# Hybrid decoder block on one core: gate projections of token groups two and three in float32r halves, gathers planned with other factors

## The chip, the cores and the metric

The kernel runs on one core of a Trainium2 chip. The metric is the device time of one execution in microseconds (us); less is better. The engines are TensorE (PE, matrix products; its weight loads are shown apart as PEld), VectorE (DVE), ScalarE (ACT), GpSimd (POOL), which here mostly issues the gathers, and SyncE (SP), which issues most loads. Each engine works through its own queue in order.

## The reference

One decoder layer over 1024 tokens of width 1024, all in float32. Three token mixers share a normalised input h; sigmoid gates merge their projections; an expert mixer follows.

```python
h = rms_norm(x, g_mix[l])
proj = h @ w_in[l]
...
y_sb = stick_breaking_attention(...) @ w_o_sb[l]
y_dil = dilated_mixture(...) @ w_o_dil[l]
y_mem = memory_attention(...) @ w_o_mem[l]
gates = jax.nn.sigmoid(h @ w_gate[l] + b_gate[l]).reshape(B, S, N_BRANCHES, D)
merged = gates[:, :, 0] * y_sb + gates[:, :, 1] * y_dil + gates[:, :, 2] * y_mem
x = x + merged @ w_out[l]
h2 = rms_norm(x, g_ffn[l])
x = x + peer_ffn(h2, w_peer_q[l], peer_subkeys[l], peer_u[l], peer_v[l])
```

In `peer_ffn` each of 8 heads of a token picks 16 of 16384 experts by product keys. For each chosen expert the row u is multiplied with h2, gelu and the softmax gate are applied, and the row v is added with that weight: 128 rows of u and 128 rows of v for each token.

## The kernel before

The 1024 tokens are eight blocks of 128. They pass through the dense part of the layer in three **groups** of two, three and three blocks (`GROUPS`, line 29). For each group `phase1` (line 1017) runs the stages one after the other: input norm, stick-breaking attention, dilated attention, memory attention, gating, output projection, second norm, expert selection. Weights come as 128 x 1024 blocks, one for each 128 output columns; `Weights` keeps three of them prepared in four buffers `w`.

**Two ways of multiplying.** A plain float32 product goes through `mm` (line 112) and leaves two records on PE, with its time at 4 cycles a column in the planner. In the other way both operands are split by `halves` (line 276): ACT copies the operand to float32r, which rounds it (hi), and DVE subtracts that from the operand (lo). Three products hi x hi, lo x hi and hi x lo then replace the one, through `mmr` (line 1193), one record each. `proj_T` (line 343) does either, by the type of the weight it gets. Only group one (`SPLIT`, line 42) uses halves in phase one; they are held in the gathers' row buffers u and v, which are idle until the first block is selected. The dense expert stage uses halves too.

**Gating** (`gating`, line 775) goes over eight column blocks and three branches. For each of the 24 pairs it computes the gate projection of h (1024 rows, eight products), Tanh on ACT, then the branch's own projection with w_o out of `oT` (four, two or four products), and combines the two on DVE. It yields after each of the two. `out_proj` follows.

**Experts.** Blocks 4 and 6 (`DENSE`) are computed densely, against all 16384 experts, by `dense` (line 1245) after the three groups. The other six blocks gather. A **step** is one u row and one v row for 128 partitions: two indirect DMAs on POOL, a product with sum on DVE (line 1151), and four PE products (line 1177). A block has 128 steps, so there are 768. PE's four times four products of four steps stand together, followed by two products that spread the next tokens' h2 (line 1090). There are five buffers for u rows and six for v rows, and a gather waits until its buffer is free.

**The planner** (the loop at the end of `block_kernel`) decides where in the program steps stand. It holds two clocks: `pe`, to which each piece of phase one adds its estimated PE time times `slow` and each step adds 700 ns, and `dma`, to which each adds its bytes by `bw`. While `dma` is ahead it takes another piece of phase one (or of the dense stage), otherwise a step. `SLOW` (line 39) has 1.38 for phase one and 1.1 for the dense stage, `BW` (line 38) 295 and 360 GB/s. So a smaller factor on a stage puts fewer steps into it, and a higher rate puts more steps into every stage. The scheduler below the planner keeps the written order on ACT and may move instructions of the other engines a little.

**The gate matrix** (`gate_matrix`, line 1203) builds the dense blocks' gates. For block 4 this happens during gating and output projection of group three, one or two pieces at each yield of these stages. It stages 1 MB tiles from `room` (line 1197), out of the pool `big` with three buffers, and stores them to memory; for block 6 they come from a pool with two buffers, `g`.

Other names: `qpad` (line 222) holds the padded queries of the attentions; its zero halves are written once. `k0`, `v` of the pool `kvp` are keys and values of the nearest dilated group, `pT` transposed probabilities; all are unused during gating. `sc` holds the selection's scores.

Of the kernel before, what the change touches and what calls it, by code (L numbers as in the profile page):

```python
# [7 lines left out]
F32 = mybir.dt.float32  # L8
# [29 lines left out]
BW = 295.0, 360.0  # L38
SLOW = 1.38, 1.1
# [38 lines left out]
def block_kernel(ctx: ExitStack, tc: tile.TileContext, io):  # L78
# [143 lines left out]
    qpad = const.tile([128, 6, NMAX], F32)  # L222
    for i in range(6):
        h0 = 64 if i % 2 == 0 else 0
        nc.vector.memset(qpad[h0:h0 + 64, i, :], 0.0)
# [25 lines left out]
    def weight_order(gidx):  # L251
# [9 lines left out]
        for pp in range(2):  # L261
            for g in range(3):
                for x in range(3):
                    yield "w_in", NB_SB + 6 * x + 2 * g + pp, every, split and x < 2
            for h in range(2):
                yield "w_in", NB_SB + 18 + 2 * pp + h, every, split
        for n in range(8):
            for br, (k0, nk) in enumerate(BR):
                yield "w_gate", br * 8 + n, every, split
                yield "w_o", n, slice(k0, k0 + nk), False  # L270
# [72 lines left out]
    def proj_T(w, h, n):  # L343

        p = bank()
        if type(w) is tuple:
            wh, wl = w
            for k in range(KD):
                hh, hl = (x[:, k % 4, :n] for x in h[1][k // 4])
                mmr(p[:, :n], wh[:, k, :], hh, start=k == 0, stop=False)  # L350
                mmr(p[:, :n], wl[:, k, :], hh, start=False, stop=False)
                mmr(p[:, :n], wh[:, k, :], hl, start=False, stop=k == KD - 1)
            return p
# [3 lines left out]
        return p  # L357

# [6 lines left out]
    def both(gidx, h, n):  # L365
# [4 lines left out]
        for k in range(0, KD, 4):  # L370
            parts.append(tuple(x.rearrange("p (k n) -> p k n", k=4) for x in spare()))
            halves(*(x[:, :, :n] for x in parts[-1]), (h[0] if type(h) is list else h)[:, k:k + 4, :n])
        return h, parts

# [44 lines left out]
    def stick_breaking(pipe, weights, hT, n0, G, oT):  # L419
        N = G * 128  # L420
        t0 = n0 * 128
# [127 lines left out]
    def dilated(pipe, weights, hT, n0, G, oT, between):  # L549
        N = G * 128  # L550
        t0 = n0 * 128
# [223 lines left out]
    def gating(pipe, weights, hT, N, oT, mT):  # L775

        for n in range(8):
            for br, (k0, nk) in enumerate(BR):
                p = proj_T(weights("w_gate", br * 8 + n), hT, N)
# [237 lines left out]
    def phase1(gidx, n0, G, out):  # L1017
# [34 lines left out]
        yield from out_proj(weights, mT, n0, G, x2)  # L1052
        h2T = [big.tile([128, 8, NS], F32, name="big") for _ in subs(G)]
# [143 lines left out]
    def room():  # L1197
# [3 lines left out]
        return big.tile([128, 64, 32], F32, name="big")  # L1201
# [186 lines left out]
    def rest():  # L1388
        n0 = built = 0
        odd = False  # L1390
        for g in range(len(GROUPS)):
            for stage in phase1(g, n0, GROUPS[g], ready):
                if stage and built < ND:
# [103 lines left out]
```

## Time and profile before

| | us |
|---|---|
| median of three runs | 3574.66 |
| lowest and highest run | 3574.15, 3581.68 |
| the profiled execution | 3564.13 |
| its span, first to last instruction | 3562.4 |

In the page's slices below, each column is a fortieth of the span (89 us) and each digit a busy share in tenths; the last row is what the DMA engines moved.

```profile
PE   6999879989999889999998999776779999999954
DVE  5444597565644469995656665788867677777654
DMA  4425659999899999989998999998999999999999
GB/s 151 140 84 182 221 210 342 336 342 340 318 405 392 403 361 348 331 329 356 328 351 292 391 386 401 350 326 338 399 384 391 365 382 382 390 383 373 349 380 377
```

Until about 484 us group one runs, with no gathers. Then follow group two with the first gathers (to 1387 us), group three (to 2411 us), the rest of the gate matrix (to 2652 us), the dense stage, and from 3396 us the gathers that are left. These borders are read from the first products of each stage on PE.

### The profile page before, as it was taken

What the parts mean: (1) busy time and instruction counts of PE and PEld (TensorE: products, weight loads), DVE (VectorE), ACT (ScalarE), POOL (GpSimd) and SP (SyncE); (2) the same over time, 40 slices, a digit from 0 to 9 for tenths busy, and PEclk for the clock granted to TensorE, in tenths of its full rate; (3) what the DMA queues carried; (4) which work ended last, traced back from release to release, by engine and by line L of the source; (5) the groups of instructions that cost most, each with busy time, mean ns of one, the idle gap of its engine ahead of it and who ended that gap; (6) DMA issues with size and microseconds to landing.
All of it is one profiled execution on the core that took longest, in us unless ns stands there. A gap on an engine that the chain in (4) does not pass through costs nothing.

```text
span 3562.4 us, 61070 instructions
## 1 busy us (share of the span) xinstructions
PE 3189.3 (90%) x22930; PEld 2359.5 (66%) x22930; DVE 2356.0 (66%) x6003; ACT 1371.6 (39%) x2747; POOL 1768.1 (50%) x1544
## 2 busy tenths in 40 slices
PE   6999879989999889999998999776779999999954
PEld 6889856656555766666565657654558888888720
DVE  5444597565644469995656665788867677777654
ACT  4443345554411214656544221322224444444410
POOL 0000036655566565766555655566645444544476
PEclk9989989999999999999999999887899999999965
DMA  4425659999899999989998999998999999999999
GB/s 151 140 84 182 221 210 342 336 342 340 318 405 392 403 361 348 331 329 356 328 351 292 391 386 401 350 326 338 399 384 391 365 382 382 390 383 373 349 380 377
DMA packets 346431, 1185.56 MB, mean 333 GB/s; under 512 B 38744, under 2 KB 80216, under 8 KB 326680
## 3 DMA queue, kind: packets, MB, share of 16 engines
q0 software_dynamic: 221184, 805.40, 59.6%
q1 hardware_dynamic: 102672, 337.95, 25.9%
q10 hardware_dynamic: 22280, 38.31, 2.8%
q8 instruction: 181, 2.97, 0.3%
q14 instruction: 114, 0.93, 0.1%
HBM read 1142.18 MB, written 39.32 MB: 332 GB/s over the span
## 4 chain that ended last, share of the span: by engine, by line
PE 60%; DVE 14%; DMA 14%; issue 5%; ACT 4%; POOL 2%; ACTq 0%; SPq 0%; POOLq 0%; DVEq 0%
PE bank L117 30%; PE bank L1195 21%; DMA u<-in_u,iT 7%; PE po L1177 7%; DVE u L1151 4%; DMA v<-in_v,iT 2%; PE pb L1090 2%; DMA b3d<-sp 1%; PE bank L121 1%; POOL u L1097 1%; POOL v L1097 1%; ACT L126 1%; DMA g<-gd 1%; ACT e L128 1%; DMA gd<-g 1%
## 5 line engine op out<-in xcount | busy, mean ns | idle before, releaser
L1097 POOL DMA_INDIRECT u<-in_u,iT x768 | 920.9, 1199 | 965.0 <-DVE i L865 487.7
L1097 POOL DMA_INDIRECT v<-in_v,iT x768 | 846.4, 1102 | 817.8 <-PE po L1177 644.5
L1151 DVE SCALAR_TENSOR_TENSOR u<-u,hb 128x1024 f32<-128x1024 f32 x768 | 927.0, 1223 | 437.6 <-ACT hb L128 274.3
L1177 PE MATMUL po<-v,wz 128*32 128x256 f32 x6144 | 443.7, 416 | 150.2 <-DMA v<-in_v,iT 83.2
L117 PE MATMUL bank<-wide,w 128*128 128x384 f32 x1536 | 520.8, 493 | 2.6 <-DMA w<-in_w_gate 2.6
L117 PEld LDWEIGHTS bank<-wide,w 128*128 128x128 f32 x1536 | 293.1, 193 | 202.7 <-issue 11.2
L1177 PEld LDWEIGHTS po<-v,wz 128*32 128x32 f32 x6144 | 181.8, 115 | 369.6 <-DMA v<-in_v,iT 115.7
L128 ACT ACTIVATE hb<-pb 128x512 f32<-128x512 f32 x384 | 208.2, 595 | 400.0 <-PE pb L1090 257.3
L117 PEld LDWEIGHTS bank<-w,wide 128*128 128x128 f32 x2304 | 263.0, 192 | 7.5 <-issue 2.3
L117 PE MATMUL bank<-w,wide 128*128 128x128 f32 x2304 | 265.3, 275 | 0.2 <-DMA w<-in_w_out 0.2
L1195 PE MATMUL bank<-hh,ul 128*128 128x256 f32 x848 | 240.0, 283 | 1.3 <-DVE ul L1275 1.3
L1195 PE MATMUL bank<-hh,uh 128*128 128x256 f32 x848 | 240.9, 284 | 0.0
L1195 PE MATMUL bank<-hl,uh 128*128 128x256 f32 x848 | 239.9, 283 | 0.0
L128 ACT ACTIVATE e<-bank 128x512 f32<-128x512 f32 (+2 forms) x208 | 109.6, 527 | 277.4 <-PE bank L117 249.3
L1195 PE MATMUL bank<-vh,wh 128*128 128x512 f32 x512 | 203.0, 403 | 2.2 <-ACT vh L128 2.2
L1195 PE MATMUL bank<-vl,wh 128*128 128x512 f32 x512 | 201.8, 394 | 2.4 <-DVE vl L1275 2.3
L1195 PE MATMUL bank<-vh,wl 128*128 128x512 f32 x512 | 199.5, 390 | 0.0
L126 ACT ACT_TABLE_LOAD x144 | 184.8, 1283 | 20.6 <-issue 8.4
L128 ACT ACTIVATE w<-bank 128x256 f32<-128x256 f32 x128 | 49.3, 385 | 366.0 <-PE bank L1195 285.1
L1275 DVE TENSOR_TENSOR vl<-vr,vh 128x1024 fp32r<-128x1024 f32 x128 | 157.1, 1227 | 31.8 <-ACT vh L128 31.8
L117 PE MATMUL bank<-big,w 128*128 128x128 f32 (+1 forms) x1024 | 175.9, 330 | 0.6 <-DMA w<-in_w_pq 0.6
L1195 PE MATMUL bank<-u 128*128 128x256 f32 x544 | 164.9, 303 | 10.2 <-ACT u L128 10.2
(297 smaller groups left out, 5887.9 us busy)
## 6 DMA issues: line engine op xcount, KB each, us to landing
ur<-in_uT SPq DMA_DIRECT2D x64, 1024.0 KB
vr<-in_vd SPq DMA_DIRECT2D x64, 1024.0 KB
w<-in_w_in SPq DMA_DIRECT2D x102, 512.0 KB
w<-in_w_gate SPq DMA_DIRECT2D x72, 512.0 KB
w<-in_w_pq SPq DMA_DIRECT2D x48, 512.0 KB
g<-gd SPq DMA_DIRECT2D x16, 1024.0 KB
w<-in_w_o SPq DMA_DIRECT2D x48, 256.0 KB
w<-in_w_out SPq DMA_DIRECT2D x24, 512.0 KB
```

What stands on the lines that cost most here:

```text
L117: nc.tensor.matmul(out, lhsT, rhs, **kw)
L121: nc.tensor.transpose(out, in_, ident)
L126: nc.scalar.preload_act_table_set(s)
L128: nc.scalar.activation(out, in_, f, **kw)
L1090: nc.tensor.matmul(pb, which[:, jj].rearrange("p q s -> p (q s)"), box["b3"][:, f], start=True, stop=True)
L1097: nc.gpsimd.indirect_dma_start(out=t, out_offset=None, in_=io[kind], in_offset=bass.IndirectOffsetOnAxis(ap=ap, axis=0))
L1151: nc.vector.scalar_tensor_tensor(u, u, 1.0, self.hb, op0=OP.mult, op1=OP.mult, accum_out=self.parts[:, i:i + 1])
L1177: nc.tensor.matmul(po[32 * k:32 * k + 32, h:h + 256], wz[:, i, :], v[:, 256 * k:256 * k + 256], start=jj == 0 and i == 0, stop=jj == QB - ...
L1195: nc.tensor.matmul(out, lhsT, rhs, **kw)
L1275: nc.vector.tensor_sub(lo, r[:, x], hi)
```

## The change

The gate projections of groups two and three are split into halves, all but the first of each group. The tokens' halves (`gate_tokens`) take three tiles of `big` and one of `sq`. The weights' halves (`gate_halves`) go by turns into the tile of `qpad` and into `k0`, `v` and two tiles `pT`. The weight of the next projection is split ahead of the present one, so a gate weight is loaded one place earlier. `qpad`'s zero halves are written anew after the output projection of group two. `room` takes its tiles from `sc`, which has two buffers, since `big` is taken. The planner's first rate becomes 330 GB/s, and its factor becomes 1.0 in gating and output projection (stages that yield 1); the other stages keep 1.38.

```diff
-BW = 295.0, 360.0
-SLOW = 1.38, 1.1
+BW = 330.0, 360.0
+SLOW = 1.38, 1.1, 1.0
...
+    def query_pad():
+
+        held_q[0] = const.tile([128, 6, NMAX], F32, name="qpad")
+        for i in range(6):
+            h0 = 64 if i % 2 == 0 else 0
+            nc.vector.memset(held_q[0][h0:h0 + 64, i, :], 0.0)
+        return held_q[0]
...
+        gate_blocks = [("w_gate", br * 8 + n, every, split) for n in range(8) for br in range(3)]
+        if not split:
+            yield gate_blocks.pop(0)
         for n in range(8):
-            for br, (k0, nk) in enumerate(BR):
-                yield "w_gate", br * 8 + n, every, split
+            for k0, nk in BR:
+                if gate_blocks:
+                    yield gate_blocks.pop(0)
                 yield "w_o", n, slice(k0, k0 + nk), False
...
+    def gate_tokens(hT, N):
+
+        a, b, c = (big.tile([128, 2048], F32, name="big").bitcast(F32R) for _ in range(3))
+        sq = tmp.tile([128, NMAX], F32, name="sq").bitcast(F32R)
+        rows = lambda t, o, m: t[:, o:o + m * NMAX].rearrange("p (k n) -> p k n", k=m)
+        hi = ((rows(a, 0, 5), 0, 5), (rows(b, 0, 3), 5, 3))
+        lo = ((rows(b, 3 * NMAX, 2), 0, 2), (rows(c, 0, 5), 2, 5), (rows(sq, 0, 1), 7, 1))
+        his, los = [], []
+        for t, k, m in hi:
+            actf(t[:, :, :N], hT[0][:, k:k + m, :N], AF.Copy)
+            his += [t[:, x] for x in range(m)]
+        for t, k, m in lo:
+            los += [t[:, x] for x in range(m)]
+            for x in range(m):
+                nc.vector.tensor_sub(t[:, x, :N], hT[0][:, k + x, :N], his[k + x][:, :N])
+        return hT[0], list(zip(his, los))
+
+    def gate_halves(j, w):
+
+        four = lambda t: t.rearrange("p (k c) -> p k c", c=128)
+        if j % 2:
+            flat = const.tile([128, 6, NMAX], F32, name="qpad").rearrange("p s n -> p (s n)").bitcast(F32R)
+            return halves(*(flat[:, x * 1024:x * 1024 + 1024].rearrange("p (k c) -> p k c", k=8) for x in range(2)), w)
+        hi = [four(kvp.tile([128, 512], F32, name="k0").bitcast(F32R)),
+              kvp.tile([128, 4, 128], F32, name="v").bitcast(F32R)]
+        lo = [four(tmp.tile([128, 512], F32, name="pT").bitcast(F32R)) for _ in range(2)]
+        for x in range(2):
+            halves(hi[x], lo[x], w[:, 4 * x:4 * x + 4])
+        return hi, lo
...
     def gating(pipe, weights, hT, N, oT, mT):
 
+        whole = hT[1] is None
+        index = [br * 8 + n for n in range(8) for br in range(3)]
+        if whole:
+            near = weights("w_gate", index[0]), hT
+            hT = gate_tokens(hT, N)
+        j = 0
         for n in range(8):
             for br, (k0, nk) in enumerate(BR):
-                p = proj_T(weights("w_gate", br * 8 + n), hT, N)
+                if whole:
+                    (w, h), j = near, j + 1
+                    if j < 24:
+                        near = gate_halves(j, weights("w_gate", index[j])), hT
+                else:
+                    w, h = weights("w_gate", br * 8 + n), hT
+                p = proj_T(w, h, N)
...
         yield from out_proj(weights, mT, n0, G, x2)
+        if gidx not in SPLIT and n0 + G < NT:
+            query_pad()
...
-        return big.tile([128, 64, 32], F32, name="big")
+        return sc.tile([128, 16, 128], F32, name="sc").rearrange("p a b -> p (a b)") \
+            .rearrange("p (b t) -> p b t", t=32)
...
             for stage in phase1(g, n0, GROUPS[g], ready):
+                slow[0] = SLOW[2 if stage == 1 else 0]
```

`proj_T` takes the tokens' halves as a list by k, and the weights' halves as one tile or a list of two. Line numbers behind these places grow by up to 64: line 1177 becomes 1239, line 1195 becomes 1257, line 1151 becomes 1213.

How the programs' order changes is shown at three places. The first is PE in the gating of group two. `po` is a lump of four steps, `oT,w` a w_o product, `wide,w` eight plain products of a gate projection. Before:

```order
L1090 MATMUL pb<-b_8676,which 128x512
L117 MATMUL bank<-wide,w 128x384 x8
L117 MATMUL bank<-oT,w 128x384 x4
L117 MATMUL bank<-wide,w 128x384 x8
L1177 MATMUL po<-v,wz 32x256 x16
```

In the changed kernel, with `big` and `sq` holding the tokens' halves and `qpad`, `k`, `v`, `pT` those of the weights:

```order
L1152 MATMUL pb<-b_8201,which 128x512
L117 MATMUL bank<-oT,w 128x384 x4
L1257 MATMUL bank<-big,qpad 128x384 x23
L1257 MATMUL bank<-sq,qpad 128x384
L117 MATMUL bank<-oT,w 128x384 x4
L1257 MATMUL bank<-big,k_9010 128x384
L1257 MATMUL bank<-big,pT 128x384
```

Eight float32 products became 24 in float32r, and fewer step lumps stand between the projections. Counted over the stage, four products of `po` to a step, there are 60 steps before and 36 now in this gating, and 68 and 40 in that of group three.

The second place is DVE at the start of the same gating. `u,parts` is a step's product with sum, `wide<-e,bank` and `e<-e,bank` combine a gate with its branch. Before:

```order
L1151 SCALAR_TENSOR_TENSOR u,parts<-u,hb 128x1024
L789 SCALAR_TENSOR_TENSOR wide<-e,bank 128x384
L1165 TENSOR_TENSOR gel<-gel,gT 128x4
L1151 SCALAR_TENSOR_TENSOR u,parts<-u,hb 128x1024
L1166 TENSOR_TENSOR wz<-gel,spread 128x128
L1151 SCALAR_TENSOR_TENSOR u,parts<-u,hb 128x1024 x3
L792 SCALAR_TENSOR_TENSOR e<-e,bank 128x384
```

Now, where line 405 makes the tokens' lo and line 290 the weights':

```order
L405 TENSOR_TENSOR big<-wide,big 128x384 x7
L405 TENSOR_TENSOR sq<-wide,big 128x384
L290 TENSOR_TENSOR qpad<-w,qpad 128x1024
L1213 SCALAR_TENSOR_TENSOR u,parts<-u,hb 128x1024
L849 SCALAR_TENSOR_TENSOR wide<-e,bank 128x384
L290 TENSOR_TENSOR pT<-w,k_8883 128x512
L290 TENSOR_TENSOR pT<-w,v 128x512
L1227 TENSOR_TENSOR gel<-gel,gT 128x4
L1213 SCALAR_TENSOR_TENSOR u,parts<-u,hb 128x1024
```

The subtractions stand between the steps' products, one weight (1024 columns) for each projection.

The third place is PE in the stick-breaking attention of group three, around an input projection (`wide,w`). Before:

```order
L117 MATMUL bank<-sp,none 128x256
L117 MATMUL bank<-wide,w 128x384 x8
L117 MATMUL bank<-e,big 64x128 x4
L1177 MATMUL po<-v,wz 32x256 x16
L1090 LDWEIGHTS which
L1090 MATMUL pb<-b_12038,which 128x512
```

Now:

```order
L1239 MATMUL po<-v,wz 32x256 x4
L117 MATMUL bank<-sp,ntri 128x256
L117 MATMUL bank<-S,none 128x256
L117 MATMUL bank<-sp,none 128x256
L117 MATMUL bank<-wide,w 128x384 x2
L1239 MATMUL po<-v,wz 32x256 x4
L117 MATMUL bank<-wide,w 128x384 x6
```

The steps' products stand apart, four at a time, and closer together. The attention of group two has 116 steps before and 136 now, that of group three 148 and 176; output projection to selection of group two keeps 56, and all that follows the gating of group three goes from 320 to 324.

More of the change, by code (lines that the diff above doesn't have):

```diff
@@ L221, in block_kernel @@
     nc.vector.tensor_scalar(gs[:, 1:2], gq_mem, 128.0 ** -0.5, None, op0=OP.mult)
[L222 to L225, printed above, removed]
+    held_q = [None]
+    def query_pad():
[5 more added lines that the diff above has]
+    query_pad()
     c_sbk = dram.tile([4, 128, T], F32, name="c_sbk")
@@ L348, in proj_T @@
             for k in range(KD):
[L349 to L352, printed above, removed]
+                hh, hl = (x[:, :n] for x in h[1][k])
+                mmr(p[:, :n], block_of(wh, k), hh, start=k == 0, stop=False)
+                mmr(p[:, :n], block_of(wl, k), hh, start=False, stop=False)
+                mmr(p[:, :n], block_of(wh, k), hl, start=False, stop=k == KD - 1)
             return p
@@ L357, in proj_T, with block_of @@
         return p
+    def block_of(w, k):
+        return w[k // 4][:, k % 4, :] if type(w) is list else w[:, k, :]
     def pieces(h, n):
@@ L370, in both @@
         for k in range(0, KD, 4):
-            parts.append(tuple(x.rearrange("p (k n) -> p k n", k=4) for x in spare()))
-            halves(*(x[:, :, :n] for x in parts[-1]), (h[0] if type(h) is list else h)[:, k:k + 4, :n])
+            hi, lo = (x.rearrange("p (k n) -> p k n", k=4) for x in spare())
+            halves(*(x[:, :, :n] for x in (hi, lo)), (h[0] if type(h) is list else h)[:, k:k + 4, :n])
+            parts += [(hi[:, x], lo[:, x]) for x in range(4)]
         return h, parts
+    def gate_tokens(hT, N):
[24 more added lines that the diff above has]
+        return hi, lo
     def head_norm(p, n, dim, lhs, done):
@@ L420, in stick_breaking @@
         N = G * 128
+        qpad = held_q[0]
         t0 = n0 * 128
@@ L550, in dilated @@
         N = G * 128
+        qpad = held_q[0]
         t0 = n0 * 128
@@ L1052, in phase1 @@
         yield from out_proj(weights, mT, n0, G, x2)
+        if gidx not in SPLIT and n0 + G < NT:
+            query_pad()
         h2T = [big.tile([128, 8, NS], F32, name="big") for _ in subs(G)]
```

## The prediction

> **What bounds the kernel now.** I read the page first, for the engines and the DMA rings over the whole span, then cut the span at the stages and asked for each engine's busy time there.
>
> ```profile
> span 3562.4 us, 61070 instructions
> PE 3189.3 (90%) x22930; PEld 2359.5 (66%) x22930; DVE 2356.0 (66%) x6003; ACT 1371.6 (39%) x2747; POOL 1768.1 (50%) x1544
> PE bank L117 30%; PE bank L1195 21%; DMA u<-in_u,iT 7%; PE po L1177 7%; DVE u L1151 4%; DMA v<-in_v,iT 2%; PE pb L1090 2%; DMA b3d<-sp 1%; PE bank L121 1%; POOL u L1097 1%; POOL v L1097 1%; ACT L126 1%; DMA g<-gd 1%; ACT e L128 1%; DMA gd<-g 1%
> q0 software_dynamic: 221184, 805.40, 59.6%
> ```
>
> TensorE is busy nine tenths of the time, and the chain that ended last runs through it, through line 117 (float32 products) most of all. The last row is the expert gathers alone: 59.6% of sixteen engines' time for 768 steps, so one step (one u row and one v row for 128 experts, 805.40/768 = 1.05 MB) costs 0.596 x 3562.4 / 768 = **2.76 us of all DMA engines**. The next view is by stage. Columns after the length: busy time of PE, weight load, DVE, ACT, POOL, then the granted clock, the DMA share, GB/s.
>
> ```profile
> 484.00:941.00 457.00, 421.02 (x3222) 279.84 (x3211) 303.22 (x804) 234.09 (x431) 275.42 (x245) 0.96 0.90 333
> 941.00:1153.00 212.00, 210.95 (x1058) 118.38 (x1053) 102.64 (x201) 34.26 (x74) 136.43 (x123) 1.00 1.01 389
> 1153.00:1387.00 234.00, 204.59 (x1580) 163.65 (x1579) 144.96 (x437) 54.86 (x144) 131.28 (x120) 0.94 1.00 385
> 1387.00:1922.00 535.00, 500.50 (x3909) 335.30 (x3911) 402.09 (x1151) 306.80 (x542) 323.06 (x288) 0.96 0.90 327
> 1922.00:2164.00 242.00, 238.45 (x1331) 146.46 (x1332) 151.23 (x373) 61.97 (x184) 141.99 (x131) 0.99 0.99 382
> 2164.00:2411.00 247.00, 201.34 (x1672) 163.82 (x1670) 181.09 (x688) 59.38 (x160) 136.91 (x121) 0.88 0.93 349
> 2411.00:2652.00 241.00, 174.24 (x1112) 121.02 (x1112) 190.81 (x606) 62.87 (x199) 147.97 (x123) 0.86 0.99 380
> 3396.00:3562.00 166.00, 81.53 (x581) 18.85 (x572) 84.06 (x159) 18.00 (x46) 119.15 (x118) 0.56 0.98 385
> ```
>
> In order: attention of group two, its gating, its output and selection; the same three of group three; the gate matrix; the tail after the dense stage. **In both gatings PE is full (99%) and DMA is full too** (share 1.01 and 0.99). In both attention stages PE has 36 and 34.5 us idle, and DMA has a tenth to spare. So the gating has PE work to lose and too many gathers; the attention has DMA time to take them.
>
> **The projections.** The chain in group two's gating gives the prices there, the records of the dense stage those of float32r.
>
> ```profile
> 996.40 12.90 PE bank L117 x40
> 1009.30 1.86 PE po L1177 x32
> 1011.17 0.54 PE pb L1090 x2
> ```
>
> ```profile
> 3000.09 0.28 PE L1195 MATMUL bank<-hh,uh 128*128 128x256 f32 x1
> ...
> 3002.96 0.40 PE L1195 MATMUL bank<-vh,wh 128*128 128x512 f32 x1
> ...
> 3005.71 0.28 PE L1195 MATMUL bank<-hh,uh 128*128 128x256 f32 x1
> ```
>
> A float32 product of 384 columns leaves two records; 40 records take 12.90 us, 0.3225 us each, so a projection of eight products is 16 x 0.3225 = 5.16 us. In float32r there are 24 products with one record each. From 3000.09 to 3002.96 stand 24 starts of 256 columns, 0.120 us apart; from there to 3005.71 twelve of 512, 0.229 us apart. The trace has none of 384; half way between is 0.174 us, with these two as the ends. A projection is then 24 x 0.174 = 4.19 us (2.9 to 5.5). It saves 0.97 us, and the 23 of 24 that are split save **22 us a group**. The weight products of line 117 with oT stay float32.
>
> The Trainium skill (TensorE: Matmul & The Clock Gate, Back-to-back issue gap) gives N/2.4 + 2.5 ns for warm products. That would be 109 and 216 ns for the two widths; the rows show 120 and 229, so the rows decide. By its formula 384 columns take 162.5 ns, and the estimate would be 6.5 us better in each group.
>
> **What feeds them.** Each split weight adds an ACT copy and a DVE subtraction; the same pair stands in group one.
>
> ```profile
> L128 ACT ACTIVATE u<-w 128x1024 fp32r<-128x1024 f32 x68 | 71.5, 1053 | 49.7 <-DMA w<-in_w_pq 25.3 <-DMA w<-in_w_gate 9.7 <-DVE big L587 3.7
> L279 DVE TENSOR_TENSOR v<-w,u 128x1024 fp32r<-128x1024 f32 x68 | 82.9, 1222 | 76.8 <-ACT u L128 76.2
> L1151 DVE SCALAR_TENSOR_TENSOR u<-u,hb 128x1024 f32<-128x1024 f32 x768 | 927.0, 1223 | 437.6 <-ACT hb L128 274.3 <-DMA u<-in_u,iT 162.2
> L794 DVE TENSOR_TENSOR wide<-wide,e 128x384 f32<-128x384 f32 x15 | 8.4, 560 | 0.3
> ```
>
> That is 23 x 1.05 = 24 us of ACT and 23 x 1.22 = 28 us of DVE a group, plus the tokens: 3 us of ACT (three times 1024 columns) and 8 x 0.56 = 4.5 us of DVE. ACT had 178 us idle in this gating, DVE 109. The split of weight j+1 is written ahead of product j, so its cover is one projection and one w_o product, 4.19 + 4 x 0.3225 = 5.5 us at least, against 2.3 us of its own. In DVE's order up to three expert products stand between two subtractions (four once in group three), 3.7 us; that is over the 3.2 us left, but where so many stand, PE's order has a lump of a step group too, 2.4 us. I cost the split at nothing; without that cover it is up to 1 us on each of 46 projections. The tokens (first copy to last subtraction some 6 us) lie under the unsplit first projection and its w_o product (5.16 + 2.58 us); I take 3 us a group for engines that are late there, 0 to 8.
>
> **The gathers move.** Counting the products of line 1177 in the two programs' order, four a step: attention of group two has 116 steps before and 136 now, its gating 60 and 36, output and selection 56 and 56, attention of group three 148 and 176, its gating 68 and 40. The stages behind have 320 before and 324 now. On PE a step is a quarter of 1.86 + 0.54, 0.60 us. So, from the profiled execution:
>
> - gating of group two: -22 - 24 x 0.60 = -36.7 us;
> - gating of group three: -22 - 28 x 0.60 = -39.1 us;
> - attention of group two: PE 421 + 12 = 433 us, with the 36 us idle kept 469; DMA 0.90 x 457 + 20 x 2.76 = 466 us at share 1. The larger gives +12 us (+0 if the idle takes the steps in, +33 if DMA holds only 0.95);
> - attention of group three: PE 500.5 + 17 + 34.5 = 552 us; DMA 0.90 x 535 + 28 x 2.76 = 559 us; +24 us (+0, or +53 at 0.95). DVE has 402 us there and gets 28 x 1.4 = 39 more, still under 559;
> - four steps later: up to 4 x 2.76 = 11 us where DMA is full, as in the last two rows of the stages; I take 5.
>
> **Buffers and queues.** The gate matrix of block four, built during group three's gating, now stages in two buffers of the selection's scores (`sc`) rather than three of `big`. Block six uses the same code with two:
>
> ```profile
> L128 ACT ACTIVATE big<-bank 128x128 f32<-128x128 f32 x128 | 36.4, 420 | 57.6 <-PE bank L117 57.6
> L128 ACT ACTIVATE g<-bank 128x128 f32<-128x128 f32 x128 | 35.8, 423 | 44.3 <-DMA gd<-g 28.8 <-PE bank L117 15.3
> ```
>
> With three, ACT never waited for a store; with two, 28.8 us in all. Behind that wait on ACT stand the gates' Tanh and the next weight copy, and for these PE. The generator's steps lie further apart in the gating, so most of the wait passes: 2 us, 0 to 14. On SP's queue the group's x rows are now fetched early in the gating, because the first `wide` tile is free after the tokens are split, and each w_gate one place sooner; no engine waits longer for it, since the gating loses 25 to 30 MB of gathers. The six memsets of the padded queries are 0.38 us each on a DVE with half its time free.
>
> ```profile
> L225 DVE MEMSET qpad<- x6: 378/378/378, 1.3 to 4.3; 64x384 f32 x6
> ```
>
> **The sum:** -36.7 - 39.1 + 12 + 24 + 5 + 6 (starts) + 2 = -27, rounded to **-28 us** on the profiled execution: 3564.1 to 3536 us. The median of the runs shown is 3574.7, 10.5 above the profiled one; from it the forecast is **3547 us**.
>
> **The rivals.**
>
> *The attention swallows the steps* (better). PE is idle there for 36 + 34.5 us and the added steps need 29 us of it; if their products fall into that idle time they cost nothing, and the last column shows DMA at 385 to 389 GB/s elsewhere. Then only 5 + 6 + 2 stand against -76: -63 us, 3512. Against: at the stage's own mix DMA must rise from 0.90 to 1.02.
>
> *No gain, DMA at a lower ceiling.* If a stage of mixed, small transfers holds only 0.97, the two attentions take (466 + 559)/0.97 = 1057 us, 65 more than now, which with 13 cancels the -76: 3574. For it: neither stage shows more than 0.90 today. Against: 0.99 with PE as the bound in the gate matrix and dense stages. The Trainium skill (DMA: Bandwidth & Descriptors, Where 436 GB/s comes from) has 358 GB/s bind a core's transfers with memory. This trace disagrees, 389 GB/s over 212 us. By that rule the attentions, at 152 + 21 and 175 + 29 MB, would take 484 and 571 us, and the sum would be about zero.
>
> *Slower.* The same place at 0.95 or less: 1079 us, +87 - 76 + 13 = +24 us, 3598. It decides from 0.97 down. PE then waits at products of line 1177 for v rows.
>
> *The halves come late* (the split doesn't save what it says): from 1 us on each of 46 projections, the 44 us are gone and the sum is +18 us, 3593. For it: the three and four expert products between two subtractions, and in group three the gate matrix's work on the same engine. Against: DVE would be busy 151 - 28 x 1.4 + 33 = 145 of 203 us there, and less in group two.
>
> **How the numbers follow.** Forecast (-45 to -12 us) 0.45; swallowed steps 0.20; no gain 0.20; slower attention 0.10; late halves 0.05. A measurement of this kernel can tell about 0.2%, 7 us, from no change. Faster takes the first two and a little of the third: 0.67; same 0.18; slower 0.15. Range: from 3505 (the better rival with a few us of waits gone) to 3590, which holds the no-gain case and part of the slower one.
>
> **What would show it.** Records of 384 columns in float32r starting 0.17 to 0.18 us apart; gatings of some 175 and 203 us with DMA near 0.85; attentions of about 469 and 559 us with DMA near 1.00; the dense stage as long as before. It is wrong if the attentions grow by over 65 us together (look for waits of line 1177 for v), if PE waits in the gating for the halves of w, or if the start spacing is above 0.21 us, where a split projection costs as much as the old one.

## The result, and the profile after

| | before | after |
|---|---|---|
| median, four runs each (us) | 3576.07 | 3623.38 |
| lowest and highest run | 3574.15, 3581.68 | 3616.89, 3627.97 |
| the profiled execution | 3564.13 | 3616.89 |
| its span | 3562.4 | 3615.1 |

The changed kernel is slower: ratio 1.014, 95% interval 1.0128 to 1.0152. The forecast of 3547 us was 76 us too low, and the range ended at 3590.

Out of the page of the changed kernel, first its span and engines, then the gather queue:

```profile
span 3615.1 us, 62022 instructions
PE 3207.2 (89%) x23298; PEld 2405.7 (67%) x23298; DVE 2413.5 (67%) x6093; ACT 1444.3 (40%) x2837; POOL 1781.7 (49%) x1544
q0 software_dynamic: 221184, 805.40, 59.2%
```

The gathers move the same 805.40 MB. PE is busy for 18 us more than before, although its projections were made cheaper. The stages tell where that came from. Here the borders are read to a tenth of a us from the first products of a stage on PE, and stand about 1 us behind them at most in both kernels; the attention of group three begins with the norm of its tokens, so it starts some 25 us earlier than in the prediction's table. Columns: window, length, busy time of PE, weight load, DVE, ACT, POOL, then granted clock, DMA share, GB/s. Before, from the attention of group two to the tail:

```profile
484.30:941.40 457.10, 421.12 (x3200) 279.74 (x3197) 303.05 (x803) 234.09 (x431) 275.71 (x246) 0.96 0.90 334
941.40:1155.40 214.00, 212.95 (x1066) 120.12 (x1067) 103.54 (x202) 34.26 (x74) 137.93 (x125) 1.00 1.01 389
1155.40:1361.60 206.20, 181.37 (x1486) 151.65 (x1484) 120.44 (x369) 48.33 (x133) 119.06 (x109) 0.95 1.00 385
1361.60:1923.10 561.50, 522.01 (x4015) 345.95 (x4016) 426.68 (x1220) 313.34 (x554) 334.58 (x297) 0.95 0.90 329
1923.10:2171.30 248.20, 245.06 (x1360) 150.84 (x1361) 154.38 (x381) 65.17 (x193) 145.68 (x136) 0.99 1.00 383
2171.30:2378.30 207.00, 182.23 (x1464) 153.50 (x1463) 144.73 (x553) 46.26 (x132) 118.41 (x104) 0.92 0.97 367
2378.30:2650.10 271.80, 184.60 (x1253) 126.01 (x1251) 222.17 (x726) 70.89 (x217) 160.38 (x134) 0.83 0.95 361
2650.10:3400.40 750.30, 744.40 (x5317) 630.86 (x5318) 535.31 (x829) 346.42 (x574) 359.76 (x277) 1.00 0.98 376
3400.40:3562.40 162.00, 77.13 (x541) 15.90 (x539) 81.66 (x156) 17.26 (x45) 115.73 (x114) 0.55 0.98 388
```

After, the same stages:

```profile
482.90:983.90 501.00, 456.97 (x3370) 282.45 (x3363) 328.29 (x854) 250.15 (x456) 316.56 (x285) 0.95 0.94 348
983.90:1159.50 175.60, 175.60 (x1050) 139.79 (x1049) 102.41 (x186) 52.43 (x91) 90.27 (x78) 1.00 0.93 343
1159.50:1380.30 220.80, 190.78 (x1488) 153.73 (x1486) 120.67 (x378) 46.58 (x133) 116.02 (x106) 0.92 0.92 345
1380.30:1985.10 604.80, 555.38 (x4251) 345.56 (x4252) 460.79 (x1283) 332.89 (x583) 392.71 (x350) 0.95 0.95 352
1985.10:2196.60 211.50, 205.88 (x1306) 168.65 (x1306) 151.59 (x355) 82.38 (x208) 96.13 (x85) 0.98 0.91 334
2196.60:2407.40 210.80, 185.74 (x1464) 153.00 (x1464) 141.03 (x553) 49.00 (x135) 115.39 (x104) 0.93 0.93 345
2407.40:2688.10 280.70, 188.68 (x1270) 128.45 (x1268) 228.09 (x733) 71.43 (x219) 175.30 (x141) 0.83 0.95 363
2688.10:3449.10 761.00, 750.16 (x5332) 634.42 (x5333) 534.91 (x832) 345.76 (x573) 361.49 (x276) 0.99 0.97 370
3449.10:3615.10 166.00, 81.23 (x541) 16.38 (x539) 81.95 (x156) 18.09 (x46) 116.99 (x116) 0.52 0.98 383
```

Length after minus length before, with the forecast's term beside it:

| stage | measured | forecast |
|---|---|---|
| attention, group two | +44 | +12 |
| gating, group two | -38 | -37 and 3 for the start |
| output and selection, group two | +15 | 0 |
| attention, group three | +43 | +24 |
| gating, group three | -37 | -39, 3 for the start, 2 for the buffers |
| all behind it | +4, +9, +11, +4 | +5 |

The two gatings gave 75 us, as forecast, and DMA is no longer full in them (share 1.01 and 1.00 before, 0.93 and 0.91 now). All other stages together gave back 129. Two traces of one kernel differ by up to 4 us in a stage, so the two terms of +4 are no more than that by themselves; a second trace of the changed kernel has +4, +10, +14 and +3 in the last row. The two attentions took the steps at 44/20 = 2.2 us and 43/28 = 1.5 us each, where their products on PE are 0.60 us. DMA stands at 0.94 and 0.95 there, not at 1.

### The profile page after: what moved, and what is told of

Read it like the earlier page. It is cut to its first block, busy times and chain, and to the rows that moved or that the text cites. A ratio compares the mean times of both kernels' runs of the same rounds, so it can differ in the third digit from the quotient of the medians.

```text
span 3615.1 us, 62022 instructions
## 1 busy us (share of the span) xinstructions
PE 3207.2 (89%) x23298; PEld 2405.7 (67%) x23298; DVE 2413.5 (67%) x6093; ACT 1444.3 (40%) x2837; POOL 1781.7 (49%) x1544
## 3 DMA queue, kind: packets, MB, share of 16 engines
q0 software_dynamic: 221184, 805.40, 59.2%
## 4 chain that ended last, share of the span: by engine, by line
PE 42%; DVE 9%; DMA 8%; issue 5%; ACT 2%; POOL 2%; ACTq 0%; POOLq 0%; SPq 0%; DVEq 0%
PE bank L1257 19%; PE bank L117 16%; PE po L1239 6%; DVE u L1213 3%; DMA v<-in_v,iT 2%; DMA u<-in_u,iT 2%; PE pb L1152 1%; DMA gd<-g 1%; DMA g<-gd 1%; POOL u L1159 1%; POOL v L1159 1%; DMA b3d<-sp 1%; DMA vr<-in_vd 1%; ACT hb L128 0%; ACT e L128 0%
## 5 line engine op out<-in xcount | busy, mean ns | idle before, releaser
L1159 POOL DMA_INDIRECT v<-in_v,iT x768 | 855.3, 1114 | 810.3 <-PE po L1239 621.5
L1239 PE MATMUL po<-v,wz 128*32 128x256 f32 x6144 | 481.9, 425 | 141.3 <-DMA v<-in_v,iT 79.0
L1239 PEld LDWEIGHTS po<-v,wz 128*32 128x32 f32 x6144 | 169.6, 116 | 384.2 <-DMA v<-in_v,iT 117.4
L117 PE MATMUL bank<-wide,w 128*128 128x384 f32 x800 | 286.2, 503 | 1.6 <-DVE wide L350 1.6
L117 PEld LDWEIGHTS bank<-wide,w 128*128 128x128 f32 x800 | 149.5, 194 | 115.5 <-issue 27.8
L117 PE MATMUL bank<-big,w 128*128 128x128 f32 (+1 forms) x1024 | 184.5, 336 | 0.0
L117 PEld LDWEIGHTS bank<-big,w 128*128 128x128 f32 x1024 | 161.9, 195 | 28.7 <-issue 10.3
```

What stands on the lines that cost most here:

```text
L117: nc.tensor.matmul(out, lhsT, rhs, **kw)
L1159: nc.gpsimd.indirect_dma_start(out=t, out_offset=None, in_=io[kind], in_offset=bass.IndirectOffsetOnAxis(ap=ap, axis=0))
L1239: nc.tensor.matmul(po[32 * k:32 * k + 32, h:h + 256], wz[:, i, :], v[:, 256 * k:256 * k + 256], start=jj == 0 and i == 0, stop=jj == QB - ...
```

## The experiments

The kernel before takes 3571 to 3573 us (medians) beside each group of these runs but one, which is named. Ratios are to the kernel before on the same chip. Stage times are read from the traces at the borders above; where a text below gives two values, the borders leave 2 or 3 us open. "Pieces" are runs of `po` products that stand together on PE: in the two attentions the kernel before has 39 and 48 of them in its written order, more than half of them 16 products long, and the changed kernel 103 and 118, most of them four products long.

### The split or the plan

The first run has the split with the planner's numbers of before.

```diff
-BW = 330.0, 360.0
-SLOW = 1.38, 1.1, 1.0
+BW = 295.0, 360.0
+SLOW = 1.38, 1.1, 1.38
```

> The float32r split with its buffers, but the planner's numbers of before (295 GB/s, 1.38 everywhere in phase one). Steps: attentions 116 and 144, gatings 48 and 56, all behind group three's gating 348 (320 before). Theories A and B alike: attentions as before (457 and 530 us), gatings 212 - 22 - 7 = 183 and 242 - 22 - 7 = 213 us, and 28 steps more in the dense part, which cost 0 to 28 x 2.76 = 77 us: 3505 to 3585. If the halves came late (theory C) the gatings would be above 200 and 230 us.

Measured: 3598.0 us, ratio 1.008 (1.0056 to 1.0104). Its two gatings and its tail:

```profile
951.60:1135.20 183.60, 183.28 (x1164) 142.74 (x1164) 114.51 (x212) 52.02 (x97) 115.56 (x99) 1.00 1.00 384
1906.50:2124.80 218.30, 213.84 (x1440) 172.21 (x1439) 167.53 (x390) 86.21 (x219) 122.36 (x106) 1.00 0.97 371
3356.00:3592.60 236.60, 115.20 (x779) 22.78 (x778) 117.13 (x220) 25.30 (x64) 172.13 (x172) 0.53 0.99 392
```

Each gating is 27 to 30 us shorter and PE is without a pause in the first: the halves are not late. But on the planner's clock a projection is now shorter while a step's transfers are not, so fewer steps find room, and the tail gets 92 instead of 64. It grows by 75 us, 2.7 us for each of the 28 steps, with DMA full. The attentions took 463 and 555 us with 116 and 144 steps, so they stay within 7 us of the kernel before. The split alone also loses, and by more than the 3585 us that were expected at most.

The second run is the kernel before with only the new numbers.

```diff
-BW = 295.0, 360.0
-SLOW = 1.38, 1.1
+BW = 330.0, 360.0
+SLOW = 1.38, 1.1, 1.0
...
+                slow[0] = SLOW[2 if stage == 1 else 0]
```

> The kernel before with the planner's new numbers alone, gate projections in plain float32. Steps: attentions 136 and 176 (101 and 115 pieces), gatings 48 and 48, all behind 304. Theories A and B: attentions as long as in the changed kernel, about 500 and 590 us; gatings 205 and 230 us. The stages behind lose 16 steps, up to 44 us. In all 3600 to 3645, so slower than before. If instead the split made the attentions longer (its buffers, not the plan), they are 457 and 535 us here and the time is below 3560.

Measured: 3669.25 us, ratio 1.0275 (1.0251 to 1.03). The two attentions:

```profile
483.90:980.90 497.00, 451.91 (x3377) 280.63 (x3369) 330.75 (x858) 250.28 (x456) 322.04 (x285) 0.95 0.94 349
1409.90:2033.00 623.10, 562.62 (x4257) 349.69 (x4258) 464.81 (x1289) 332.16 (x585) 396.13 (x357) 0.96 0.94 345
```

They have 136 and 176 steps, as in the changed kernel, and grow by 40 and 59 to 62 us without any split. So the attentions' growth comes from the steps put there, not from the buffers of the split. Why the second grows more here than in the changed kernel (43 us) stays open. In the gating of group two 12 steps fewer gave only 9 us.

### Scattered products, or rows that come late

Theory A: the scheduler scatters the products in fours and each piece costs PE a change between two shapes of product. Theory B: the v rows come too late at this density of steps, and the scattering is only how the scheduler meets it. For A, the products of a step group were kept together by multiplying the last row first, in the changed kernel and in the kernel before.

```diff
-                self.behind.append([gelu, weights, lambda: [sums(x) for x in range(4)]])
+                def whole_sums(sums=sums):
+                    rows = [self.vs.pop(0) for _ in range(4)]
+                    for x in (3, 0, 1, 2):
+                        sums(x, rows)
+                self.behind.append([gelu, weights, whole_sums])
```

> The changed kernel, with the four v rows of a step group multiplied in the order 4, 1, 2, 3, so that the last to land comes first and the sixteen products of line 1239 stay together: in PE's order the attention of group two has 38 pieces of them in place of 103 (34 groups), that of group three 44 in place of 118; step counts stay 136 and 176. Theory A (the scattered pieces cost PE time): the attentions fall from 502 and 592 us to about 475 and 562, the time by some 50 us to 3570. Theory B (DMA holds no more than a share of 0.95 in the attention): they stay within 8 us of 502 and 592, PE waits for v rows instead, the time stays at 3615 to 3625.

> The kernel before with the same order 4, 1, 2, 3 of the v rows. Pieces: 39 to 36 and 48 to 48 in the attentions, 54 to 31 between group three's gating and the dense stage. Theory A: no change in the attentions, 23 pieces less at some 0.2 us, so 0 to -10 us. Theory B: no change, within 7 us of before.

Measured: in the changed kernel 3639.41 us, ratio 1.0203 (1.0169 to 1.0238); in the kernel before 3607.5 us, ratio 1.0098 (1.0075 to 1.0122). The attentions of the first, by stage, and below them a row of PE's waits in the second attention (total, times, longest):

```profile
482.60:973.10 490.50, 436.15 (x3370) 290.08 (x3367) 327.96 (x854) 249.39 (x454) 318.25 (x286) 0.94 0.94 355
1374.30:1989.00 614.70, 541.16 (x4253) 358.29 (x4254) 463.82 (x1288) 331.97 (x583) 404.58 (x354) 0.94 0.93 349
```

```profile
PE po L1239 <- DMA v<-in_v,iT: 22.1, 11, 5.9
```

With the products together PE is busy 21 and 14 us less than in the changed kernel, so the 65 and 74 pieces that are gone had cost it 0.2 to 0.3 us each. But its idle time rises by 10 and 24 us, and the stages come out 10 us shorter and 10 us longer. A alone is not the cause: without the pieces PE waits for rows, and what it gains in the first attention it loses in the second. The order itself costs too, which was not expected: in the kernel before it made the tail 17 us longer (179 instead of 162), the gate matrix 11 and the first attention 8.

For B, the rows were cut to half: each gather fetches half a row, DVE multiplies that half twice, PE the same half for two quarters of the output. Half of each expert row is left out of the computation.

```diff
-            nc.gpsimd.indirect_dma_start(out=t, out_offset=None, in_=io[kind],
+            nc.gpsimd.indirect_dma_start(out=t[:, :512], out_offset=None, in_=io[kind].rearrange('e (a d) -> (e a) d', a=2),
...
-                                         v[:, 256 * k:256 * k + 256], start=jj == 0 and i == 0,
+                                         v[:, 256 * (k % 2):256 * (k % 2) + 256], start=jj == 0 and i == 0,
```

> The changed kernel with gathers of half the bytes: each indirect DMA brings 512 of a row's 1024 columns, and the products on DVE (two of 512) and PE read that half twice, so their work and the step counts stay (136 and 172 in the attentions, 40 and 47 pieces). It leaves out half of each expert row. The nearest run with whole groups is that of the order 4, 1, 2, 3: 491 and 615 us. Theory B (the attention is held by the rows' arrival): 421 + 12 + 36 = 470 and 522 + 15 + 40 = 577 us. Theory D (a step costs its time on DVE, ACT and PE in the attention, whatever the rows): both within 8 us of 491 and 615.

> The kernel before with gathers of half the bytes in the same way (half of each expert row left out). Step counts 116 and 148 in the attentions, 60 and 68 in the gatings, as before. Theory B: the rows are no bound there at a share of 0.90, so the attentions stay at 457 and 561 us and the gatings at 214 and 248; the tail of 64 steps falls from 162 to under 110 us. If the attentions fall by over 10 us each, the rows' arrival cost time before already.

Measured, one time each: 3439.6 us changed, 3465.46 us before. The two attentions of the changed kernel with half rows, then those of the kernel before with half rows and its tail:

```profile
482.90:943.30 460.40, 429.20 (x3374) 283.49 (x3367) 337.14 (x1134) 249.46 (x454) 292.29 (x286) 0.96 0.71 219
1321.70:1883.30 561.60, 521.33 (x4224) 348.48 (x4221) 471.38 (x1634) 332.92 (x582) 362.15 (x351) 0.98 0.69 214
```

```profile
482.80:922.20 439.40, 413.29 (x3204) 277.03 (x3197) 312.96 (x1043) 234.01 (x431) 246.75 (x246) 0.97 0.66 203
1332.80:1873.90 541.10, 510.65 (x4016) 341.68 (x4016) 436.31 (x1515) 313.29 (x554) 309.07 (x297) 0.97 0.63 194
3298.90:3463.70 164.80, 78.34 (x541) 16.60 (x539) 87.74 (x276) 17.27 (x45) 120.58 (x115) 0.54 0.67 195
```

With half the bytes the order of changed and before turns round: the changed kernel is 26 us faster. Its attentions fall by 41 and 43 us. Its products stand together again in this run (40 and 47 pieces), so that fall holds the price of the pieces too; beside the run that keeps them together with whole rows, half the bytes took 30 and 53 us. In the kernel before the attentions fall by 18 and 20 us, 10 and 9 of it idle time of PE, so **rows already cost time there, at a DMA share of 0.90**. What remains between the two half-row kernels is 21 us for 20 steps and 21 us for 24 (in the second attention this kernel has 172 steps, not 176), 0.9 to 1.1 us each against the 0.60 of their PE products. So of some 43 us in each attention about half hangs on the rows' bytes, with the pieces that go with them, and about half comes with the steps even when rows are cheap. One more thing is mixed into this: the granted clock in the second attention is 0.98 with half rows and 0.95 in the changed kernel, 0.97 and 0.95 in the kernel before, and some of PE's lower busy time (by 8 and 11 us in the kernel before) may be that.

Theory A was tried from the other side too: in the kernel before, each v row's products as a piece of its own everywhere.

```diff
-                self.behind.append([gelu, weights, lambda: [sums(x) for x in range(4)]])
+                self.behind.append([gelu, weights, *(lambda x=x, f=sums: f(x) for x in range(4))])
```

> The kernel before with the products of the four v rows of a group issued one row at a time, one at each of four following steps, so that they always stand in pieces of four: 90 and 122 pieces in the attentions (39 and 48 before), steps unchanged. Theory A (a piece more costs PE about 0.33 us): PE busy in the attentions 421 + 17 = 438 and 522 + 24 = 546 us, the attentions about 474 and 585. Theory B alone: PE busy and the attentions stay within 6 us of 457 and 561.

Measured: 3625.54 us, ratio 1.0155 (1.0138 to 1.0172). The two attentions and the dense stage:

```profile
485.60:933.10 447.50, 426.09 (x3200) 269.14 (x3197) 302.81 (x803) 234.63 (x431) 271.35 (x246) 0.98 0.93 340
1367.40:1926.20 558.80, 535.17 (x4015) 333.57 (x4016) 426.68 (x1216) 313.83 (x554) 328.74 (x297) 0.98 0.90 330
2672.20:3453.20 781.00, 775.15 (x5303) 619.68 (x5306) 535.89 (x829) 346.45 (x574) 362.69 (x276) 1.00 0.96 362
```

The attentions are 10 and 3 us shorter than before, although PE is busy 5 and 13 us more for 51 and 74 more pieces (0.1 to 0.2 us each). The loss lies elsewhere: the dense stage, which has no idle time for it, takes 781 us, 31 more for about 96 more pieces, 0.3 us each. The granted clock is mixed into the first two figures: it was 0.98 in these attentions, against 0.96 and 0.95 before. If PE's busy time goes with it, an estimate, a piece costs about 0.3 us there as well, and part of what the attentions gained may be the clock. So a piece costs PE 0.2 to 0.3 us, and whether single rows buy anything by themselves where PE waits for rows is not separated from the clock.

### Table loads on ACT

The changed kernel has more switches between functions on ACT: 64 and 81 table loads in the two attentions, against 56 and 71 before. Gelu of the gathered experts was replaced by a copy (that part of the computation is left out).

```diff
-                    actf(ge, parts, AF.Gelu)
+                    actf(ge, parts, AF.Copy)
```

> The changed kernel with a copy in place of the gathered experts' gelu (left out), so that ACT needs no other function table for a step group between the exponentials of the attention. Pieces 107 and 124, steps unchanged. Theory T (the twelve more groups in the attentions cost by two table loads of 1.28 us each on ACT, which the attention waits for): the attentions fall from 501 and 605 us by over 20 us each. Theories A and B: less than 8 us each, since ACT is busy 54 and 57% there.

Measured, one time: 3614.15 us, attentions of 493 and 608 us, 8 shorter and 3 longer than in the changed kernel. There is not one table load left in them; ACT's work in the first falls from 250 to 167 us and the stage hardly moves. This theory falls.

### Other numbers for the planner, and single rows in the attentions

These four ran on a chip on which the kernel before took 3722.62 us (3703.28 to 3731.09), so only their ratios are compared. Two put fewer steps into the attentions, and three multiply single rows there alone (`apart` is set before the attentions of groups two and three and cleared before their gating).

```diff
-BW = 330.0, 360.0
-SLOW = 1.38, 1.1, 1.0
+BW = 310.0, 360.0
+SLOW = 1.38, 1.1, 1.3
...
-                self.behind.append([gelu, weights, lambda: [sums(x) for x in range(4)]])
+                self.behind.append([gelu, weights, *([lambda x=x, f=sums: f(x) for x in range(4)] if apart[0] else [lambda: [sums(x) for x in range(4)]])])
```

The kernel before with the second edit alone:

> The kernel before, with the products of the four v rows issued one row at a time in the attentions of groups two and three alone, as one whole group everywhere else. Pieces 90 and 122 in the attentions, else as before; steps unchanged. Theory B (rows freed and awaited one at a time suit a stage that is held by their arrival): the attentions fall by 10 and 3 us as in the run with single rows everywhere, the other stages stay, 3558. Theory A (pieces cost PE time first): the attentions grow by 8 us or more, over 3580.

The changed kernel with the first edit, with both, and with both and 1.38 in place of 1.3:

> The changed kernel with the planner at 310 GB/s and 1.3 in gating and output projection. Steps: attentions 124 and 157, gatings 48 and 52, output and selection of group two 59, all behind group three's gating 328 (before: 116, 148, 60, 68, 56, 320). With the prices measured so far: gatings -30 and -32 us, attentions 8 x 2.0 and 9 x 1.6 = +30 us, three steps in the selection and eight behind at up to 2.7 us +30 us: about 3570, as before. If a step cost only its 0.6 us of PE where the stage isn't full, 3530.

> The same planner numbers as the run before this one, with single rows in the attentions (100 and 133 pieces). Theory B: 10 to 20 us faster than that run, about 3555, faster than both kernels. Theory A: slower than that run.

> As the run before, with 1.38 in gating and output projection: steps 124 and 158 in the attentions, 52 and 58 in the gatings, 60 in output and selection of group two, 316 behind. Gatings 3 us longer each for four to six more steps, the stages behind up to 12 x 2.7 = 32 us shorter: 3530 to 3550 by theory B, the best so far. If the gatings are full on DMA with these steps they grow by 8 us each and the gain is half of that.

| kernel | us | ratio (95%) | attentions | gatings |
|---|---|---|---|---|
| before, single rows | 3676.01 | 0.9871 (0.9845 to 0.9896) | 485, 591 | 214, 255 |
| split, 310 and 1.3 | 3749.87 | 1.0088 (1.0062 to 1.0114) | 530, 630 | 184, 228 |
| the same, single rows | 3703.37 | 0.9951 (0.9932 to 0.997) | 510, 626 | 184, 222 |
| split, 310 and 1.38, single rows | 3686.93 | 0.9907 (0.9883 to 0.9932) | 506, 607 | 194, 228 |

With 124 and 157 steps in the attentions instead of 136 and 176 the split still loses to the kernel before. The stages of this table are read to within 4 us. Single rows won 1.2 and 1.3% in the two pairs, and the kernel before with single rows was the best, ahead of every one with the split. Whether that was the edit or this chip had to be seen on another.

### Side by side on one chip

Before, changed, and each with single rows in the attentions, on a chip on which the kernel before took 3572.64 us:

> The kernel before as a run of its own, for its stages on the same chip as the three others. All theories: ratio 1.00 within 0.3%. If this chip is like the first: attentions 457 and 561 us, DMA 0.90 in both.

> The changed kernel beside it. All theories: ratio 1.010 to 1.018, attentions 35 to 50 us longer each than in the kernel before on this chip, gatings 35 to 40 shorter.

> The kernel before with a step's four v rows multiplied one at a time in the attentions of groups two and three alone. If what it gained on the slow chip (ratio 0.987) was that chip's own, the ratio here is 0.997 to 1.003; if waiting for four rows together costs on every chip, the two attentions are 10 and 3 us shorter, as in the run with single rows everywhere, and the ratio is about 0.996.

> The same edit in the changed kernel: 129 and 163 pieces of products in the two attentions instead of 103 and 118. Transfers' own rate holds the attentions: DMA share stays at 0.94 and 0.95, the attentions stay within 5 us of the changed kernel's, ratio to it 0.998 to 1.003. Waiting for four rows together holds them: both attentions at least 10 us shorter, DMA share up to 0.96 or more, and the ratio to the kernel before 1.005 or less. The pieces themselves hold them: 3 and 5 us longer, at 0.1 us a piece.

| kernel | us | ratio (95%) | attentions |
|---|---|---|---|
| before | 3574.85 | 1.0002 (0.9987 to 1.0018) | 457, 565 |
| changed | 3621.9 | 1.0139 (1.0122 to 1.0156) | 503, 605 |
| before, single rows | 3575.55 | 1.0013 (0.9997 to 1.0029) | 450, 571 |
| changed, single rows | 3616.0 | 1.0133 (1.0113 to 1.0153) | 486, 615 |

The loss repeats. The gain of single rows does not: it belonged to the other chip. So no kernel that computes the whole layer beat the kernel before on the usual chips; the split with 310 GB/s was not run on one of them. The attentions of the changed kernel on this chip, then the same with single rows:

```profile
484.30:987.40 503.10, 456.15 (x3369) 281.31 (x3363) 328.98 (x854) 250.01 (x456) 320.51 (x285) 0.95 0.94 347
1384.60:1989.10 604.50, 554.78 (x4251) 344.65 (x4252) 460.36 (x1284) 332.92 (x583) 391.08 (x350) 0.96 0.95 352
```

```profile
484.60:970.50 485.90, 457.77 (x3364) 275.14 (x3361) 326.87 (x854) 251.41 (x456) 313.37 (x285) 0.96 0.96 360
1369.10:1984.50 615.40, 571.12 (x4243) 343.65 (x4244) 459.77 (x1282) 332.70 (x583) 386.15 (x352) 0.96 0.94 347
```

The two attentions answer differently. In the first, with 26 more pieces, PE's idle time falls from 47 to 28 us and DMA rises to 0.96: there, waiting for four rows at once looks like part of the hold (the granted clock is 0.96 in place of 0.95). In the second, with 45 more, PE is busy 16 us more and DMA does not rise. So 0.94 is not the most that the transfers can do in every such stage, and what holds the second attention at 0.95 stays open; it could be their rate or the eleven row buffers. Other numbers of row buffers were not tried.

## Why the prediction was wrong, step by step

**The projections: right.** The forecast had 0.174 us from one 384-column product in float32r to the next. The timeline of PE in the gating of group two (start, duration, line, operation, count), where rows interleave by their names:

```profile
999.72 0.51 PE L1257 MATMUL bank<-big,v 128*128 128x384 f32 x2
1000.07 0.33 PE L1257 MATMUL bank<-big,pT 128*128 128x384 f32 x1
1000.24 0.51 PE L1257 MATMUL bank<-big,v 128*128 128x384 f32 x2
1000.59 0.33 PE L1257 MATMUL bank<-big,pT 128*128 128x384 f32 x1
1000.76 0.51 PE L1257 MATMUL bank<-big,v 128*128 128x384 f32 x2
```

Three products from 999.72 to 1000.24, three more to 1000.76: 0.52/3 = 0.173 us each. The estimate of 162.5 ns by the Trainium skill's formula (TensorE: Matmul & The Clock Gate, Back-to-back issue gap) was too short here too, as for the two widths before.

**The gatings: right.** 175.6 us against 175; 211.5 against 203 on a border that stood 6 us later, so 209. Their DMA shares, 0.93 and 0.91, are above the 0.85 expected.

**The halves at nothing: right.** PE has no idle time in the first gating, and 5.6 us in the second (3.1 before). The 3 us for the start were not needed in the first; in the second, the 3 us and the 2 us for two staging buffers lie within its 5.6.

**The attentions: the step that failed.** It says "the attention has DMA time to take them", and takes +12 from PE's own work with the idle time kept, and +24 from DMA at a share of 1. Two things in it were wrong. First, DMA's tenth was not free: with half rows the kernel before gains 18 and 20 us there, 10 and 9 of it idle time of PE. Part of PE's idle time and of its busy time was already the price of late rows, so it could not be "kept" while 20 and 28 steps came on top. Second, a step costs the attention more than its products on PE, 0.60 us: 0.9 to 1.1 us even with half rows. The growth of 44 and 43 us can be cut up with the run that keeps the products together: PE's work rises by 436 - 421 = 15 and 541 - 522 = 19 us for the steps (0.75 and 0.68 each, near the 0.60; the granted clock of that run, 0.94 in both, is in it), by 21 and 14 more for the pieces, and idle time rises by 8 and 10. Keeping them together turns the pieces' part into waits, 10 us for the 21 in the first attention and 24 for the 14 in the second. That both are prices of the same thing, rows that come close behind their use, is argued and not shown. The granted clock does not explain the growth: it was 0.96 and 0.95 before and 0.95 in both after.

**"Output and selection 56 and 56", so nothing: wrong by 15 us.** The count over the stage hid that steps move inside it and come apart: in the trace, 16 steps stood in the output projection and 40 in the norm and selection behind it, in 14 pieces, now 12 and 44, in 25 pieces. The stage's DMA share fell from 1.00 to 0.92. That is not the whole cause: the split alone keeps the 16 and 40 steps and the 14 pieces, and its stage is 9 us longer as well. The rest was not tried by itself.

**Four steps later, 5 us: wrong by 22.** The stages behind took 27 us more. With half rows the dense stage takes 748 us in the changed kernel and 745 in the one before, and the gate matrix 237 and 244, so most of this part, too, goes with the rows' bytes; which of the waits carries it was not separated.

**The rivals.** That the attention swallows the steps is out: PE's idle time there did not take them in, but rose from 36 and 39 to 44 and 49 us. The slower rival, "the same place at 0.95 or less", was right in place and in size: it priced the two attentions at +87 us, and they took 44 + 43. That the size met to a us is in part luck, since its mechanism is one lower ceiling on DMA: the first attention went to 0.96 with single rows, and with half rows the added steps still cost 21 us in each. Its 3598 us fell short since it kept the forecast's 5 us for all stages but attentions and gatings, and these took 42. Its sign on PE, the waits for v rows, was wrong. In the changed kernel's second attention they are (total, times, longest):

```profile
PE po L1239 <- DMA v<-in_v,iT: 3.6, 1, 3.6
```

DVE's waits for u rows did not rise either: 21 and 16 us in the two attentions before, 17 and 10 after. As the run that keeps the products together shows, it is the scattering that hides these waits; there PE waits 11 and 22 us for v rows and DVE 50 and 44 for u rows. In the changed kernel they show as pieces, and on POOL. POOL's waits in the attention of group two, before and then after:

```profile
POOL v L1097 <- PE po L1177: 89.5, 34, 10.3
POOL u L1097 <- DVE u L1151: 9.7, 5, 3.9
```

```profile
POOL u L1159 <- DVE u L1213: 42.6, 19, 7.0
POOL v L1159 <- PE po L1239: 34.8, 27, 8.0
```

Before, POOL mostly waited for PE to free a v buffer; a reading of that is that rows lay ready. Now its waits for DVE to free a u buffer last as long, and rows seem to lie less far ahead. This rival was given 0.10; the evidence for it was in the page (no stage of this mix above 0.90), and was set against the 0.99 of the gate matrix and the dense stage. The 358 GB/s that the Trainium skill puts to a core's transfers with memory (DMA: Bandwidth & Descriptors, Where 436 GB/s comes from) was no ceiling here: the tail of the changed kernel moves 383, and the first attention with single rows 360. By that figure the attentions would have taken 484 and 571 us, an estimate, and the second 598 at the border used here. They moved 348 and 352 and took 501 and 605.

**Where the gain went.** From the first gather to the end DMA was 0.95 busy before and is now (362 and 356 GB/s over 3078 and 3132 us): the gathers fill the kernel as much as PE does. The gatings gave 75 us and put 24 + 28 = 52 steps elsewhere, 48 of them into the attentions, so the change pays only while a step costs less than 75/52 = 1.4 us where it goes. The attentions took 87/48 = 1.8 us for each, the tail of the split alone 2.7, and the stages other than attentions and gatings 42 us more.

**The sum itself.** Its terms give -26.8 us and were taken as -28; that one us changes nothing.

## What to carry to other kernels

When a stage is full on its engine and on DMA at once, count where its transfers go when its products become cheaper, and measure what they cost there before the gain is counted. A DMA share of 0.90 with idle time on the engine that consumes was not room here; cutting the bytes in half in one run, and seeing whether the stage shortens, is a way to find out. And count work that is moved inside a stage as well as between stages.

## What was not expected of the hardware

- A piece of four `po` products (32 columns of PE's array each) between full products costs PE some 0.3 us beyond its own time: 31 us for about 96 pieces more in a dense stage without idle time.
- The tail of 64 steps isn't set by bytes: 162 us with whole rows at a DMA share of 0.98, 165 us with half rows at 0.67. Multiplying a group's last row first makes it 179 us.
- One chip of the four in these experiments ran the same kernel in 3722.62 us instead of 3571 to 3573, 4% more. There the attentions of the kernel with single rows took 485 and 591 us, against 450 and 571, with DMA at 0.88 and 0.87 instead of 0.93 and 0.89, and an edit that changes nothing elsewhere gained 1.3%.
